# A two-layer hybrid attention kernel: the context side's modulation sums and one gate move from VectorE to GpSimd

## The chip, the cores and the metric

The kernel runs on one core of a Trainium2 chip. A core has TensorE (matmuls, PE in the profile, with its weight loads as PEld), VectorE (DVE), ScalarE (ACT), GpSimd (POOL), and SyncE (SP), which here issues nearly all transfers between HBM and SBUF. Each engine works through its own queue in order and waits for the others by semaphores. The metric is the device time of one execution in microseconds; less is better.

## The reference

Two layers of a backbone over 512 latent tokens and 256 context tokens of width 2048. Each layer first turns a conditioning vector into a shift, a scale and a gate, for the latent tokens from `c` and for the context tokens from `c_ctx`:

```python
sc = silu(c); scc = silu(c_ctx)
for l in range(2):
    shift, scale, gate       = split(sc  @ w_ada[l] + b_ada[l], 3)   # w_ada[l]: 2048 x 6144
    shift_c, scale_c, gate_c = split(scc @ w_ada[l] + b_ada[l], 3)
    h  = rms(x,  norm_w[l]) * (1 + scale)   + shift
    hc = rms(xc, norm_w[l]) * (1 + scale_c) + shift_c
    # h, hc -> one input projection -> three attention groups -> y (gated by silu(z))
    x = x + gate * (y @ w_out[l])
    if l == 0:
        xc = xc + gate_c * (y_c @ w_out[l])
return x
```

Everything is float32. The second layer's context output is never needed, so its `gate_c` is not either: layer 1 needs a shift and a scale for both sides, and a gate for the latent side alone.

## The kernel before, in words

Most of the time goes into matmuls with weights that stream from HBM: 128-row weight tiles land in `ws`, are split into a rounded high part `wh` (ScalarE, line 232) and the rest `wl` (VectorE, line 238), and three products of high and low parts approximate a float32 product (line 327). Between these projections the attention units run: scores into the PSUM tile `S`, a softmax over VectorE (lines 271, 276, 255) and ScalarE, transposes (line 330), and the product with the values. A `g` is a PSUM bank, `s` (tag `s3`) a large SBUF tile, `tm` and `sm` are temporaries.

The order of all instructions is made by a planner, in Python, while the program is built. Each strand of work is a generator (`Fiber`) with a priority; `Weaver` advances a clock of its own, every helper (`stt`, `ts`, `act`, `pmul`, ...) adds its estimated cost to its engine's clock with `bump`, and `gate` holds a strand until its instruction would start within 1.35 us (`AHEAD`). The result is one fixed order per engine. At run time the engines follow that order, whatever the real durations are.

The modulation of a layer is a product of one vector with a 2048 x 6144 matrix, for two vectors (sides 0, latent, and 1, context). The first layer's shift and scale are computed with TensorE (`ada_blocks`, line 734). All the rest goes through `ada_vec`: a chunk is 512 columns of `w_ada`, and an item is 128 rows of it, a tile `wa` of 128 x 512 (256 KB, two buffers). For each item and each side, VectorE multiplies `wa` by the side's activated conditioning `scT[:, k, m]` (one number per partition) and adds it into an accumulator `ac` (two buffers): a tensor_scalar (line 253) for the first of the 16 items of a chunk, a scalar_tensor_tensor (line 260) for the other 15. At the chunk's end TensorE sums over the partitions, with the accumulator as weights and a column of ones (line 792). After each item the strand pauses for `PACE` = 4 us of the planner's time.

`ada_rest` runs three such pieces one after the other at the lowest of the side priorities: layer 0's gate (4 chunks, both sides), layer 1's shift and scale (8 chunks, both sides), layer 1's gate (4 chunks, side 0). That is 16 chunks, 256 items and 448 VectorE instructions. Layer 1's shift and scale are wanted when layer 1 normalises its input; its gate is wanted by its output projection (`post_out`), near the end.

GpSimd has little to do: constants at the start, small transfers (line 308), and elementwise products (`pmul`, line 281): attention output times the silu gate, `s<-ot,s`, and two in the rotary embedding.

Of the kernel before, what the change touches and what calls it, by code (L numbers as in the profile page):

```python
# [138 lines left out]
class Kern:  # L139
# [139 lines left out]
    def pmul(self, out, a, b):  # L279
        yield from self.gate("pool")  # L280
        self.nc.gpsimd.tensor_tensor(out, a, b, op=OP.mult)  # L281
        self.w.bump("pool", 0.1 + 0.0035 * self.n(out))

    def load(self, out, in_, b=262144):

# [323 lines left out]
def body(K):  # L609
# [144 lines left out]
        K.put("tm", a)  # L754
        yield from ada_use(l, c0, n, pt, (0, 1))

    def ada_vec(l, c0s, sides):


        n = 512  # L760
        items = [(c0, k) for c0 in c0s for k in range(KT)]
        pend = deque()
        nxt = 0
        for c0 in c0s:
            acc = []
            for k in range(KT):
                while nxt < len(items) and (not pend or K.free("wa")):
                    w.cur.ft = w.vt
                    s = yield from K.get("wa")
                    c_, k_ = items[nxt]  # L770
                    nxt += 1
                    ts = yield from K.load_ahead(s, t["w_ada"][l, k_ * 128:(k_ + 1) * 128, c_:c_ + n])
                    pend.append((s, ts))
                s, ts = pend.popleft()
                yield from K.wait(ev_c)
                w.cur.ft = max(w.vt, ts)
                if k == 0:
                    for _ in sides:
                        acc.append((yield from K.get("ac")))
                for a, m in zip(acc, sides):  # L780
                    sc = scT[:, k, m:m + 1]
                    if k == 0:
                        yield from K.ts(a, s, sc, OP.mult, fast=True)
                    else:
                        yield from K.stt(a, s, sc, a, OP.mult, OP.add)
                K.put("wa", s)
                yield w.vt + PACE
            pt = yield from K.get("g")
            yield from K.sync()
            for c in range(n // 128):  # L790
                for a, m in zip(acc, sides):
                    nc.tensor.matmul(pt[:, 2 * c + m:2 * c + m + 1], a[:, c * 128:(c + 1) * 128], one,  # L792
                                     start=c == 0 and m == sides[0], stop=c == n // 128 - 1 and m == sides[-1],
                                     skip_group_check=True)
            w.pe(0.21 * n // 128 * len(sides))
            K.put("ac", *acc)
            w.spawn(ada_use(l, c0, n, pt, sides), 1, w.cur.ft)
# [24 lines left out]

    def ada_gate(l):
        sides = (0, 1) if l == 0 else (0,)
        yield from ada_vec(l, [2 * D + c for c in range(0, D, 512)], sides)
        yield from K.wait(*ev_gb[l])
        ps = yield from K.get("g")
        yield from K.sync()
        for m in sides:
            K.tr(ps[:KT, m * 128:(m + 1) * 128], ada[l][:, 32:48, m])  # L830
        w.pe(0.2)
        g = yield from K.get("tm")
        yield from K.act(g[:KT, :128 * len(sides)], ps[:KT, :128 * len(sides)])
        K.put("g", ps)
        for m in sides:
            yield from K.store(gscr[l][m], g[:KT, m * 128:(m + 1) * 128], 8192)
        K.put("tm", g)
        K.set(ev_gate[l])
# [1182 lines left out]

    def ada_rest():
        yield from ada_gate(0)
        yield from ada_vec(1, [c + o for c in range(0, D, 512) for o in (0, D)], (0, 1))
        yield from ada_gate(1)

    w.spawn(modulation(), 3)
# [69 lines left out]
```

## Time and profile before

| What | Value |
|---|---|
| Time, median of 3 runs | 2949.91 us (2947.4 to 2950.17) |
| Profiled execution: its own time | 2949.59 us |
| Profiled execution: span | 2947.8 us |
| TensorE busy | 2826.9 us (96%) |
| VectorE busy | 2025.8 us (69%) |
| ScalarE busy | 1243.7 us (42%) |
| GpSimd busy | 144.8 us (5%) |
| First and last accumulation into `ac` | 184.3 and 1634.0 us |
| Granted TensorE clock, mean | 0.99 |

The 1.8 us between the span and the execution's own time lie around the program. A row of the groups reads: line, engine, operation, output and inputs by name, shape, count, then busy time, mean of one in ns, and the idle time of the engine before them with what ended it. In the chain of work that ended last, each step is followed back to what released it; its shares tell through which lines the end of the kernel was reached. Layer 0 fills about the first 1700 us, layer 1 the rest.

### The profile page before, as it was taken

Reading aid. Unit: us, or ns where it says so; the run is one execution under the profiler, and the core shown is the slowest. Engines: PE = TensorE matmul, PEld = TensorE weight load, DVE = VectorE, ACT = ScalarE, POOL = GpSimd, SP = SyncE. Lnnn points to the kernel's source line nnn. Section 1 sums busy time; section 2 is a strip of 40 time slices with the busy share of each in tenths; the row PEclk is TensorE's granted clock in tenths of the full one; section 3 lists DMA queues with packets and bytes.
Section 4 is the critical chain, followed back from the end, with each engine's and each line's share of the span. In section 5 each row is a group of like instructions: output and inputs, shape, how many; then the busy total and the mean of one; then the engine's idle time right before and its main releaser. Section 6 shows DMA issues by size and latency. Waiting matters only on the chain.

```text
span 2947.8 us, 56481 instructions
## 1 busy us (share of the span) xinstructions
PE 2826.9 (96%) x21402; PEld 2715.2 (92%) x21402; DVE 2025.8 (69%) x5275; ACT 1243.7 (42%) x2714; POOL 144.8 (5%) x189
## 2 busy tenths in 40 slices
PE   5999999999989999889999999999999999999998
PEld 3779999999989999879999999999998999889998
DVE  5247787786987888889855374656657676489643
ACT  4223443342543454546421164444444455356421
POOL 3000000000100001000000000000000000000000
PEclk9999999999989999999999999999999999999999
DMA  9864444434323335424445343333231323412254
GB/s 254 251 203 129 120 122 116 121 109 117 101 85 106 90 111 154 149 83 129 164 140 168 113 128 86 92 96 89 71 99 46 90 61 102 132 45 88 93 160 127
DMA packets 423600, 349.19 MB, mean 118 GB/s; under 512 B 66260, under 2 KB 370178, under 8 KB 423328
## 3 DMA queue, kind: packets, MB, share of 16 engines
q1 hardware_dynamic: 421456, 344.27, 39.6%
q0 software_dynamic: 1872, 1.32, 0.5%
q8 instruction: 168, 2.75, 0.4%
q14 instruction: 104, 0.85, 0.1%
HBM read 303.97 MB, written 32.07 MB: 114 GB/s over the span
## 4 chain that ended last, share of the span: by engine, by line
PE 81%; DVE 11%; DMA 4%; issue 2%; SPq 1%; ACT 1%; DVEq 0%; ACTq 0%
PE g L327 67%; PE S L327 6%; PE g L330 5%; DVE wl L238 2%; DMA s<-w_ada 2%; SPq L297 1%; DVE s L271 1%; DVE s L238 1%; DVE ac L260 1%; DVE pt L238 1%; PE g L792 1%; DVE tm L238 1%; DVE s L260 1%; DVE s L255 1%; ACT s L232 1%
## 5 line engine op out<-in xcount | busy, mean ns | idle before, releaser
L327 PE MATMUL g<-wh,s 128*128 128x256 f32 (+1 forms) x9064 | 1766.7, 288 | 18.7 <-DVE tm L238 6.5
L327 PEld LDWEIGHTS g<-wh,s 128*128 128x128 f32 x9064 | 1457.7, 192 | 28.9 <-issue 9.1
L327 PE MATMUL g<-wl,s 128*128 128x256 f32 (+1 forms) x4532 | 1295.7, 286 | 6.5 <-DVE wl L238 6.3
L327 PEld LDWEIGHTS g<-wl,s 128*128 128x128 f32 x4532 | 870.7, 192 | 10.8 <-DVE wl L238 9.5
L238 DVE TENSOR_TENSOR wl<-ws,wh 128x512 fp32r<-128x512 f32 (+1 forms) x598 | 410.6, 687 | 455.6 <-PE g L327 262.7
L232 ACT ACTIVATE wh<-ws 128x512 fp32r<-128x512 f32 (+2 forms) x606 | 372.0, 615 | 415.5 <-PE g L327 383.7
L327 PE MATMUL g<-s,wh 128*128 128x384 f32 (+1 forms) x1600 | 453.4, 358 | 1.1 <-DVE s L238 0.6
L232 ACT ACTIVATE s<-s,sm 128x640 f32<-128x640 f32 (+3 forms) x260 | 195.9, 753 | 391.7 <-DVE sm L271 313.4
L260 DVE SCALAR_TENSOR_TENSOR ac<-wa,scT,ac 128x512 f32<-128x512 f32 x420 | 311.7, 760 | 9.2 <-DMA wa<-w_ada 8.3
L327 PEld LDWEIGHTS g<-s,wh 128*128 128x128 f32 x1600 | 294.3, 189 | 25.0 <-issue 2.1
L327 PE MATMUL g<-s,wl 128*128 128x384 f32 (+1 forms) x736 | 261.7, 356 | 0.0
L330 PE MATMUL g<-ident,s 128*128 128x128 f32 x1520 | 234.3, 279 | 20.1 <-DVE s L255 10.3
L327 PE MATMUL S<-s,s 128*128 128x256 f32 (+2 forms) x1260 | 240.6, 320 | 12.1 <-DVE sm L271 11.2
L232 ACT ACTIVATE tm<-g 128x512 f32<-128x512 f32 (+4 forms) x298 | 146.6, 513 | 226.3 <-PE g L327 126.8
L238 DVE TENSOR_TENSOR pt<-g,pt 128x512 fp32r<-128x512 f32 (+1 forms) x338 | 196.8, 591 | 65.0 <-ACT pt L232 63.8
L327 PE MATMUL g<-pt,s 128*128 128x256 f32 (+1 forms) x1348 | 223.0, 289 | 12.7 <-DVE pt L238 7.9
L232 ACT ACTIVATE pt<-g 128x512 fp32r<-128x512 f32 (+1 forms) x338 | 168.7, 516 | 142.4 <-PE g L330 134.7
L327 PEld LDWEIGHTS S<-s,s 128*128 128x128 f32 x1260 | 188.9, 191 | 27.1 <-DVE sm L271 17.9
L330 PEld LDWEIGHTS g<-ident,s 128*128 128x128 f32 x1520 | 179.7, 143 | 33.0 <-DVE s L255 13.7
L327 PEld LDWEIGHTS g<-pt,s 128*128 128x128 f32 x1348 | 188.8, 193 | 22.1 <-DVE pt L238 12.8
L281 POOL TENSOR_TENSOR s<-ot,s 64x256 f32<-64x256 f32 x100 | 87.3, 873 | 1976.9 <-DVE ot L238 1943.1
L327 PEld LDWEIGHTS g<-s,wl 128*128 128x128 f32 x736 | 139.3, 189 | 9.4
(155 smaller groups left out, 2226.3 us busy)
## 6 DMA issues: line engine op xcount, KB each, us to landing
wa<-w_ada SPq DMA_DIRECT2D x256, 256.0 KB
ws<-w_in SPq DMA_DIRECT2D x328, 128.0 KB
ws<-w_in SPq DMA_DIRECT2D x160, 256.0 KB
ws<-w_out SPq DMA_DIRECT2D x136, 256.0 KB
s<-w_ada SPq DMA_DIRECT2D x128, 256.0 KB
s<-scr SPq DMA_DIRECT2D x36, 384.0 KB
ws<-w_in SPq DMA_DIRECT2D x64, 192.0 KB
ws<-w_qb SPq DMA_DIRECT2D x54, 192.0 KB
```

Of the source, the lines that this page charges most:

```text
L232: self.nc.scalar.activation(out, in_, func, bias=bias, scale=scale, **kw)
L238: self.nc.vector.tensor_tensor(out, a, b, op=op)
L255: self.nc.vector.tensor_scalar(out, a, s1, s2, op0=op0, op1=op1)
L260: self.nc.vector.scalar_tensor_tensor(out, a, s, b, op0=op0, op1=op1)
L271: self.nc.vector.tensor_tensor_reduce(out, a, b, -1.0, init, OP.add, OP.min, acc)
L281: self.nc.gpsimd.tensor_tensor(out, a, b, op=OP.mult)
L297: self.nc.sync.dma_start(out, in_)
L327: self.nc.tensor.matmul(out, l, r, start=start, stop=stop, skip_group_check=True)
L330: self.nc.tensor.transpose(out, in_, self.ident)
L792: nc.tensor.matmul(pt[:, 2 * c + m:2 * c + m + 1], a[:, c * 128:(c + 1) * 128], one, start=c == 0 and m == sides[0], stop=c == n // 128 - ...
```

## The change

`ada_vec` takes a further argument, `pool`: the sides whose sums GpSimd computes. GpSimd gets no fused multiply-add here. For such a side, the first item of a chunk is one tensor_scalar into the accumulator (`pts`); each of the other 15 is a tensor_scalar that multiplies the tile `wa` in place, and a tensor_tensor that adds it to the accumulator (`padd`). Side 0, which reads the same tile, comes before it in program order, so the in-place product waits for VectorE's read. In layer 0's gate and in layer 1's shift and scale, side 1 goes to GpSimd; in layer 1's gate, which has only side 0, that side does. A `wa` buffer is now free for its next load when the later of both engines is done with it. In `ada_rest`, layer 1's gate waits until layer 1's input is complete.

```diff
+    def padd(self, out, a, b):
+        yield from self.gate("pool")
+        self.nc.gpsimd.tensor_tensor(out, a, b, op=OP.add)
+        self.w.bump("pool", 0.2 + 0.0025 * self.n(out))
+
+    def pts(self, out, a, s, op):
+        yield from self.gate("pool")
+        self.nc.gpsimd.tensor_scalar(out, a, s, None, op0=op)
+        self.w.bump("pool", 0.2 + 0.0025 * self.n(out))
...
-    def ada_vec(l, c0s, sides):
+    def ada_vec(l, c0s, sides, pool):
...
-                w.cur.ft = max(w.vt, ts)
                 if k == 0:
                     for _ in sides:
                         acc.append((yield from K.get("ac")))
+                end = t0 = max(w.vt, ts)
                 for a, m in zip(acc, sides):
+                    w.cur.ft = t0
                     sc = scT[:, k, m:m + 1]
-                    if k == 0:
+                    if m in pool:
+                        w.cur.ft = end
+                        yield from K.pts(s if k else a, s, sc, OP.mult)
+                        if k:
+                            yield from K.padd(a, a, s)
+                    elif k == 0:
                         yield from K.ts(a, s, sc, OP.mult, fast=True)
                     else:
                         yield from K.stt(a, s, sc, a, OP.mult, OP.add)
+                    end = max(end, w.cur.ft)
+                w.cur.ft = end
                 K.put("wa", s)
                 yield w.vt + PACE
...
-        yield from ada_vec(l, [2 * D + c for c in range(0, D, 512)], sides)
+        yield from ada_vec(l, [2 * D + c for c in range(0, D, 512)], sides, (1 - l,))
...
-        yield from ada_vec(1, [c + o for c in range(0, D, 512) for o in (0, D)], (0, 1))
+        yield from ada_vec(1, [c + o for c in range(0, D, 512) for o in (0, D)], (0, 1), (1,))
+        yield from K.wait(*(e for p in ev_in[1] for e in p))
         yield from ada_gate(1)
```

The planner makes a new order from this. First, VectorE in the first chunk of layer 0's gate, before:

```order
L260 SCALAR_TENSOR_TENSOR ac<-wa,scT,ac 128x512
L238 TENSOR_TENSOR s_2017<-s_2019,s_2016 128x256
L260 SCALAR_TENSOR_TENSOR ac<-wa,scT,ac 128x512
L260 SCALAR_TENSOR_TENSOR s_1946<-tm,g 128x384
L238 TENSOR_TENSOR wl<-ws,wh 128x512
L260 SCALAR_TENSOR_TENSOR s_1946<-tm,g 128x384
L260 SCALAR_TENSOR_TENSOR ac<-wa,scT,ac 128x512 x2
```

and in the changed program:

```order
L260 SCALAR_TENSOR_TENSOR ac<-wa,scT,ac 128x512
L238 TENSOR_TENSOR s_2017<-s_2019,s_2016 128x256
L260 SCALAR_TENSOR_TENSOR s_1946<-tm,g 128x384
L238 TENSOR_TENSOR wl<-ws,wh 128x512
L260 SCALAR_TENSOR_TENSOR s_1946<-tm,g 128x384
L260 SCALAR_TENSOR_TENSOR ac<-wa,scT,ac 128x512
```

One accumulation of the two of each item is gone from VectorE's order; what stands between is the same. Second, GpSimd in the changed program, where layer 1 begins: the last pair of the modulation, layer 1's small transfers, and the first items of its gate.

```order
L291 TENSOR_SCALAR wa<-wa,scT 128x512
L286 TENSOR_TENSOR ac<-ac,wa 128x512
L318 DMA colA<-qn_a 64x1 x2
L318 DMA colA<-kn_a 64x1 x2
...
L318 DMA sink<-sink_b 128x12
L291 TENSOR_SCALAR ac<-wa,scT 128x512
L291 TENSOR_SCALAR wa<-wa,scT 128x512
L286 TENSOR_TENSOR ac<-ac,wa 128x512
```

Before, no accumulation stood in this queue, and the gate's items came ahead of layer 1. Third, TensorE's sums over the partitions, the fifteenth chunk before:

```order
L327 MATMUL g<-wh,s_17638 128x256
L327 MATMUL g<-wl,s_17638 128x256
L327 MATMUL g<-wh,s_17639 128x256
L792 MATMUL g<-one,ac 128x1 x4
L327 MATMUL g<-wh,s_17635 128x256
```

and the twelfth and the thirteenth chunk of the changed program:

```order
L337 MATMUL g<-wl,s_17524 128x256
L337 MATMUL g<-wh,s_17525 128x256
L810 MATMUL g<-one,ac 128x1 x8
L337 MATMUL g<-wh,s_17527 128x256
...
L337 MATMUL g<-wl,s_21820 128x256
L337 MATMUL g<-wh,s_21821 128x256
L810 MATMUL g<-one,ac 128x1 x4
L337 MATMUL g<-wh,s_21789 128x256
```

The twelfth chunk, the last of layer 1's modulation, ends where the fifteenth ended before, and the gate's first chunk ends some 1900 rows later, in layer 1. The projections and attention units themselves stand in nearly the same places in TensorE's order, shifted by some tens of rows.

## The prediction

> **What bounds the kernel now.** I read the page first (busy time, then the chain of work that ended last), then the chain stage by stage, then the groups of the two accumulators, then GpSimd's own rows.
>
> ```profile
> span 2947.8 us, 56481 instructions
> PE 2826.9 (96%) x21402; PEld 2715.2 (92%) x21402; DVE 2025.8 (69%) x5275; ACT 1243.7 (42%) x2714; POOL 144.8 (5%) x189
> PE 81%; DVE 11%; DMA 4%; issue 2%; SPq 1%; ACT 1%; DVEq 0%; ACTq 0%
> ```
>
> TensorE is busy for 96% of the span and is 81% of the chain. VectorE is 69% busy, but only 11% of the chain runs through it. A microsecond taken from VectorE is therefore worth something only where the chain runs through VectorE. The sums that move lie between 184 and 1636 us; this is what each engine does there.
>
> ```profile
> core 0: us, PE busy (x) PEld busy (x) DVE busy (x) ACT busy (x) POOL busy (x), PEclk, DMA share, GB/s
> 184.00:721.00 537.00, 530.99 (x4060) 525.07 (x4057) 398.49 (x976) 198.75 (x434) 26.38 (x28) 1.00 0.42 120
> 721.00:910.00 189.00, 178.01 (x1309) 173.59 (x1308) 166.11 (x461) 88.14 (x224) 16.02 (x19) 0.95 0.32 94
> 910.00:1195.00 285.00, 277.11 (x2063) 273.75 (x2061) 237.49 (x632) 132.80 (x308) 32.23 (x39) 0.99 0.42 123
> 1195.00:1395.00 200.00, 181.80 (x1251) 170.71 (x1252) 185.96 (x554) 108.98 (x262) 1.06 (x2) 0.97 0.35 107
> 1395.00:1563.00 168.00, 161.02 (x1285) 158.14 (x1284) 113.65 (x246) 63.54 (x124) 3.22 (x5) 0.98 0.50 158
> ```
>
> Two stretches stand out. From 721 to 910 VectorE is busy for 166 of 189 us, from 1195 to 1395 for 186 of 200, and there alone TensorE has real gaps (11 and 18 us). The chain by line, for 184 to 1563 and for these two stretches:
>
> ```profile
> by line: PE g L327 63.1%; PE S L327 5.5%; PE g L330 5.3%; DVE ac L260 2.8%; DVE wl L238 2.3%; DVE s L271 2.2%; DVE s L238 2.2%; issue 1.8%; PE g L792 1.7%; DVE pt L238 1.5%; DVE s L255 1.3%; ACT s L232 1.2%; DVE s L260 1.1%; DVE tm L238 1.0
> by line: PE g L327 44.7%; DVE ac L260 7.1%; PE g L330 6.4%; DVE s L271 5.4%; PE S L327 5.1%; DVE wl L238 4.1%; DVE pt L238 3.7%; DVE s L255 3.3%; issue 3.3%; DVE tm L238 3.0%; PE g L792 2.6%; ACT s L232 1.6%; DVE ot L238 1.6%; DVE s L238 1.
> by line: PE g L327 25.0%; DVE s L238 9.9%; DVE ac L260 7.5%; DVE wl L238 6.5%; PE S L327 6.2%; PE g L330 5.0%; DVE s L260 4.9%; DVE s L271 4.9%; issue 4.8%; DVE pt L238 4.1%; DVE s L255 3.3%; DVE sm L260 2.7%; DVE sm L265 2.6%; ACT s L232 2
> ```
>
> The accumulations into `ac` are 2.8% of 1379 us, so 38.6 us of the chain, 13.4 us in the first stretch and 15.0 us in the second. That is all of their VectorE time (over 300 us) that the end of the kernel can feel today.
>
> **The change, part by part.** *What leaves VectorE.* The two groups:
>
> ```profile
> L260 DVE SCALAR_TENSOR_TENSOR ac<-wa,scT,ac x420: 730/746/1509, 189.6 to 1634.0; 128x512 f32<-128x512 f32 x140
> L253 DVE TENSOR_SCALAR ac<-wa,scT x28: 475/482/954, 184.3 to 1565.5; 128x512 f32<-128x512 f32 x28
> 184.00:721.00 537.00, 9.21 (x80) 9.45 (x81) 138.15 (x192) 1.00 0.42 120
> 721.00:910.00 189.00, 5.36 (x32) 5.33 (x33) 46.61 (x64) 0.95 0.32 94
> 910.00:1195.00 285.00, 5.88 (x52) 6.08 (x52) 70.71 (x96) 0.99 0.42 123
> 1195.00:1395.00 200.00, 3.38 (x30) 3.32 (x30) 34.82 (x48) 0.97 0.35 107
> 1395.00:1563.00 168.00, 1.90 (x16) 1.95 (x16) 23.34 (x32) 0.98 0.50 158
> ```
>
> (The last five rows are the stage view again, for instructions on `ac` alone; the third bracket counts VectorE's.) The context side of layer 0's gate (4 chunks of 16 items) and of layer 1's modulation (8 chunks), and layer 1's gate (4 chunks) are 16 chunks: 16 tensor_scalars and 240 scalar_tensor_tensors, 16 x 0.482 + 240 x 0.746 = 187 us of 2026. Before 1563 us the old kernel does 432 such instructions; the new one keeps 192 there (the latent side of 12 chunks), since by the order the twelfth chunk now ends where the fifteenth ended. So 240/432 = 56% of the 38.6 us can leave the chain: at most 21.5 us, at least nothing, if what comes next on the chain is only just behind. VectorE's other rows are ahead of TensorE in much of this time, so I take 18.
>
> *What GpSimd gets.* 256 tensor_scalars and 240 tensor_tensors of 128x512, which the old trace does not show. The nearest rows:
>
> ```profile
> L281 POOL TENSOR_TENSOR s<-ot,s 64x256 f32<-64x256 f32 x60 | 55.5, 925 | 1004.4 <-DVE ot L238 977.8 <-DVE sm L276 10.4 <-DVE sm L255 7.4
> L281 POOL TENSOR_TENSOR tm<-tm,rowB 128x384 f32<-128x384 f32 x8 | 8.7, 1093 | 39.6 <-ACT tm L232 39.6
> L281 POOL TENSOR_TENSOR tm<-tm,row_kk 128x256 f32<-128x256 f32 x4 | 3.2, 814 | 0.1
> L1998 POOL CAST maskB<-s 128x384 bf16<-128x384 f32 x1 | 0.5, 507 | 6.1 <-DMA s<-k_maskB 6.1
> ```
>
> (The first three are for 184 to 1195 us.) From 256 to 384 elements a tensor_tensor grows by 279 ns, so 512 give 1.37 us with the waits in it; undisturbed ones take 1.02 us at 384 (below), so I take 1.30. The tensor_scalar has one tensor to read: from the cast, 0.507 x 512/384 = 0.68 us below, the two-input 1.30 us above; nearer the cast, 0.7. In layer 0, 12 chunks give 192 x 0.7 + 180 x 1.3 = 368 us of GpSimd in 1379, a share of 27% beside the 6% it has. It has room; a pair of 2.0 us fits easily between items some 7 us apart. Were both 1.3 us, the share would be 35%.
>
> *What GpSimd costs VectorE.* The two engines get in each other's way today. Here are GpSimd and VectorE in the same few microseconds:
>
> ```profile
> 701.02 1.02 POOL L281 TENSOR_TENSOR tm<-tm,rowB 128x384 f32<-128x384 f32 x1 [32.62 <-ACT tm L232]
> 702.39 1.42 POOL L281 TENSOR_TENSOR tm<-tm,rowB 128x384 f32<-128x384 f32 x1 [0.35 <-ACT tm L232]
> 699.39 1.41 DVE L260 SCALAR_TENSOR_TENSOR ac<-wa,scT,ac 128x512 f32<-128x512 f32 x2
> 702.20 2.17 DVE L260 SCALAR_TENSOR_TENSOR ac<-wa,scT,ac 128x512 f32<-128x512 f32 x2
> ```
>
> The same GpSimd instruction takes 1.02 and then 1.42 us, and two accumulations that took 1.41 us before it take 2.17: each engine stood still for a while beside the other. On average, with GpSimd at work (184 to 1195) and with it idle (1410 to 1840):
>
> ```profile
> L260 DVE SCALAR_TENSOR_TENSOR ac<-wa,scT,ac 128x512 f32<-128x512 f32 x330 | 244.8, 764 | 7.3 <-DMA wa<-w_ada 6.6
> L238 DVE TENSOR_TENSOR wl<-ws,wh 128x512 fp32r<-128x512 f32 x173 | 122.0, 705 | 86.3 <-issue 57.8 <-PE g L327 16.4 <-ACT wh L232 2.7
> ...
> L238 DVE TENSOR_TENSOR wl<-ws,wh 128x512 fp32r<-128x512 f32 x96 | 66.2, 689 | 111.4 <-PE g L327 77.9 <-issue 26.0 <-ACT wh L232 6.3
> L260 DVE SCALAR_TENSOR_TENSOR ac<-wa,scT,ac 128x512 f32<-128x512 f32 x45 | 33.6, 746 | 1.9 <-DMA wa<-w_ada 1.7
> ```
>
> That is 18 and 16 ns per instruction, at a GpSimd share of (55.5 + 8.7 + 3.2)/1011 = 6.7%: 0.25 us for a share of one. At 27% it is 68 ns, and as the new instructions are some 1.3 times as long as the old ones, up to 90; I take 80 ns. Not every VectorE instruction pays; I count those that read two SBUF tensors, and tensor_scalars from SBUF to SBUF (the one on `ac` has a longest of 954 ns against a median of 482, so these wait too). On the chain from 184 to 1563 the lines `wl`, `s` L238, `s` L255 and `tm` are 6.8%, 94 us at about half a microsecond each, so 190; the remaining accumulations and the many small ones on `sm` (2.7% of 200 us at about 0.17 us are 32 in the second stretch alone) bring it to about 300. 300 x 0.08 = 24 us added, 20 if the others of a waiting set were later anyway.
>
> The Trainium skill ("SBUF — State Buffer", Who interferes with whom) states a rule against this change: VectorE and GpSimd share one pair of SBUF ports as an exclusive lock, taken by VectorE for two SBUF inputs or a two-port mode, and the second to come waits for the whole instruction. The 0.76 us that VectorE lost at 702, and the 0.40 us that GpSimd lost, agree with it.
>
> *The later gate.* Its 64 loads of 256 KB, 64 pairs on GpSimd and 16 small matmuls move from 1302-1636 to the matmuls that ran at about 1740-2043.
>
> ```profile
> by line: PE g L327 80.9%; PE g L330 5.5%; PE S L327 2.6%; DMA tm<-scr 1.8%; DMA tm<-x 1.7%; DVE wl L238 1.4%; issue 1.4%; PE g L1372 0.8%; DVE s L238 0.7%; SPq L297 0.6%; DVE s L260 0.4%; DVE tm L238 0.4%; PE g L792 0.4%; DVE pt L238 0.2%;
> ```
>
> From 1563 to 2050 lock-taking lines are about 2.5% of 487 us, some 20 instructions; GpSimd's share is there 123/300 = 41%, so 20 x 0.12 = 2.5 us more. The transfers `tm<-x` on this chain (1.7%, 8 us) share the queues with the gate's loads today; I give the move 2 us back. The gate's result is needed only by layer 1's output projection, at 2500 and later.
>
> *Buffers and queues.* `wa` has two buffers, and each is now free only after GpSimd's add. SP issues in order, so a late add would hold a weight load behind it. The planner reckons 2 x (0.2 + 0.0025 x 512) = 2.96 us for a pair that I put at 2.0, so it gives 0.96 us for waits; I cost this at nothing. The one-column matmuls L792 wait for GpSimd's last add: 16 ends, covered by the same margin; without it, a late microsecond at each end would cost TensorE 16 us. The gating products of attention (L281) now queue behind a pair, by up to 2 us; the planner counts this.
>
> **The sum.** -18 + 20 + 2.5 - 2 = +2.5 us on the profiled execution's own 2949.59 (1.8 us lies around the span): 2952, against a median of 2949.91 it is no difference. About 0.2% (5.9 us) is what a measurement here can tell from no change.
>
> **Rivals.** *No change* (forecast): 2946 to 2956. Chance 0.36.
>
> *The relief arrives, the lock costs little.* The new pairs come right after the latent side's accumulation on the same engine, at a moment when VectorE often has nothing urgent, and the planner, which knows of the lighter VectorE, places urgent work earlier. Then -21.5, a third of the lock's 24 us, and 2 us from the transfers: -15, 2935. For it: chain lines of VectorE are a tenth of the time outside the two stretches. Against: VectorE stands at 88 and 93% in them. Chance 0.32.
>
> *The lock decides: slower.* A tensor_scalar on GpSimd takes 1.3 us too, the share is 35%, and the mean wait grows with the length: 0.25 x 0.35 x 1.7 = 0.15 us on 300 instructions is 45 us, less 18, with 5 us in layer 1: +32; half of it hidden, +16. Time 2966 to 2982. Its place is 1195 to 1395, where 35 us of `ac` halve but every other instruction waits; it decides from a pair of 2.4 us, or when `wl` takes more than 0.8 us on average. The planner knows nothing of these waits, so TensorE's order leaves no room for them. Chance 0.26.
>
> *GpSimd late for its own consumers: slower.* Blocked by VectorE, a pair takes over 3 us, SP holds weight loads behind `wa`, and L792 waits: 12 to 16 ends at 2 us are up to 32 us, 2980. The two-microsecond slack of the pair speaks against it. Chance 0.06.
>
> **From these the numbers.** Faster 0.32, same 0.36, slower 0.32. The likeliest case alone is 2946 to 2956; as both signs hold most of the chance, the range runs to the middle of the faster and of the slower case: 2932 to 2974.
>
> **What would show it.** Right: VectorE's busy time falls by less than 187 us, by some 187 - 100; `wl` takes about 0.77 us on average before 1563; GpSimd is busy for about 640 us; `ac` on the chain falls to about 17 us while `wl`, `s` and `sm` gain as much. Wrong towards faster: `wl` stays near 0.70 us, and the gaps of TensorE in 721-910 and 1195-1395 (29 us together) close by half. Wrong towards slower: SP's or TensorE's waits for GpSimd's adds, or pairs over 2.4 us.

## The result: 1% slower

| | before | changed |
|---|---|---|
| Time, median of 4 runs each on the same chip | 2950.04 us (2947.4 to 2954.57) | 2980.55 us (2977.82 to 2984.5) |
| Profiled execution, its own time | 2949.59 us | 2984.5 us |

The ratio is 1.0104 (95% interval 1.0090 to 1.0118): 30.5 us slower, against a forecast of 2952 and a range up to 2974. The page of the changed kernel: span, busy times, and the two large new groups on GpSimd (POOL).

```profile
span 2982.3 us, 57007 instructions
PE 2838.3 (95%) x21402; PEld 2715.0 (91%) x21402; DVE 2001.9 (67%) x5019; ACT 1243.9 (42%) x2714; POOL 901.2 (30%) x685
...
L291 POOL TENSOR_SCALAR wa<-wa,scT 128x512 f32<-128x512 f32 x240 | 404.6, 1686 | 696.4 <-DVE ac L260 423.3
...
L286 POOL TENSOR_TENSOR ac<-ac,wa 128x512 f32<-128x512 f32 x240 | 322.8, 1345 | 19.6
```

VectorE (DVE) lost 256 instructions, and its busy time fell by 24 us, from 2025.8 to 2001.9. GpSimd is busy for 901 us, not the 640 foreseen: a pair takes 1.69 + 1.35 = 3.03 us. The tile view of `ac` gives the shortest, the median and the longest of one (ns), and when they ran:

```profile
L286 POOL TENSOR_TENSOR ac<-ac,wa x240: 1262/1295/1843, 190.1 to 2069.3; 128x512 f32<-128x512 f32 x120
L291 POOL TENSOR_SCALAR ac<-wa,scT x16: 1565/1570/1977, 182.4 to 1996.1; 128x512 f32<-128x512 f32 x16
```

The add is 1.30 us, as taken. The tensor_scalar is 1.57 us at the median, more than twice what I took, so a pair has 2.87 us even without waits. Where VectorE's time went is seen in its groups, by shape, before:

```profile
L238 DVE TENSOR_TENSOR wl<-ws,wh 128x512 fp32r<-128x512 f32 x544 | 380.7, 700 | 442.9 <-PE g L327 253.4 <-issue 130.4 <-ACT wh L232 29.9
L238 DVE TENSOR_TENSOR pt<-g,pt 128x512 fp32r<-128x512 f32 x258 | 174.1, 686 | 54.8 <-ACT pt L232 53.9
...
L255 DVE TENSOR_SCALAR s<-s,sm 128x640 f32<-128x640 f32 x80 | 44.4, 555 | 1.6
...
L238 DVE TENSOR_TENSOR sm<-sm 128x1 f32<-128x1 f32 x120 | 19.9, 166 | 25.6 <-ACT sm L232 25.0
```

and in the changed kernel:

```profile
L238 DVE TENSOR_TENSOR wl<-ws,wh 128x512 fp32r<-128x512 f32 x544 | 414.6, 762 | 480.8 <-PE g L337 285.8 <-issue 118.3 <-ACT wh L232 35.4
L238 DVE TENSOR_TENSOR pt<-g,pt 128x512 fp32r<-128x512 f32 x258 | 173.4, 684 | 53.9 <-ACT pt L232 52.9
L260 DVE SCALAR_TENSOR_TENSOR ac<-wa,scT,ac 128x512 f32<-128x512 f32 x180 | 136.7, 760 | 1.7 <-DMA wa<-w_ada 1.3
L255 DVE TENSOR_SCALAR s<-s,sm 128x640 f32<-128x640 f32 x80 | 53.0, 662 | 2.1
...
L238 DVE TENSOR_TENSOR sm<-sm 128x1 f32<-128x1 f32 x120 | 31.1, 259 | 37.3 <-ACT sm L232 36.6
```

`wl`, which reads two SBUF tensors, went from 700 to 762 ns. That is the mean over the whole kernel, and the pairs run only up to 2071 us. The same group from 184 to 1563 us alone, before and then changed:

```profile
L238 DVE TENSOR_TENSOR wl<-ws,wh 128x512 fp32r<-128x512 f32 x212 | 148.8, 702 | 108.8 <-issue 67.3 <-PE g L327 26.3 <-ACT wh L232 5.7
```

```profile
L238 DVE TENSOR_TENSOR wl<-ws,wh 128x512 fp32r<-128x512 f32 x211 | 173.7, 823 | 143.2 <-issue 64.0 <-PE g L337 54.0 <-ACT wh L232 12.6
```

So beside the pairs it takes 823 ns, and after 2080 us, without them, 700 again. Even a two-input instruction on one column (`sm`) went from 166 to 259 ns over the whole kernel. `pt<-g,pt`, which has one of its two inputs in PSUM (`g`), didn't change. One such place in the timeline (start, duration, engine; the bracket is idle time before):

```profile
1242.36 0.55 DVE L238 TENSOR_TENSOR wl<-ws,wh 128x384 fp32r<-128x384 f32 x1
...
1243.67 1.56 POOL L291 TENSOR_SCALAR wa<-wa,scT 128x512 f32<-128x512 f32 x1 [9.33 <-DVE ac L260]
1243.82 0.74 DVE L260 SCALAR_TENSOR_TENSOR s<-g,colC,s 128x512 fp32r<-128x512 f32 x1
...
1244.66 0.59 DVE L255 TENSOR_SCALAR sm<-sm 128x6 f32<-128x6 f32 x1
1245.29 0.17 DVE L253 TENSOR_SCALAR sm<-sm 128x6 int32<-128x6 int32 x1
1245.32 1.27 POOL L286 TENSOR_TENSOR ac<-ac,wa 128x512 f32<-128x512 f32 x1
1245.40 1.61 DVE L238 TENSOR_TENSOR wl<-ws,wh 128x384 fp32r<-128x384 f32 x1
...
1247.06 0.44 PE L337 MATMUL g<-wl,s 128*128 128x384 f32 x1 [1.34 <-DVE wl L238]
```

GpSimd's product ends at 1245.23; a VectorE tensor_scalar of six elements per partition, begun 1.0 us behind it, ends then too, after 0.59 us (its neighbour on as many takes 0.17). The add ends at 1246.59; `wl`, which took 0.55 us when it ran 3 us earlier, takes 1.61 us and ends 0.42 us behind the add, and the matmul that wants it starts late. The instruction on `g` at 1243.82 runs beside GpSimd undisturbed.

**Where the time arises.** The three products run the same 18732 matmuls on one line (327 before, 337 after), so I aligned the traces on the n-th of them. Each column is a kernel's time minus before's time at the same matmul, in us; the last four are experiments, told of below:

| before's time | changed | e1, no pairs | e10, sums on VectorE | e8, gate on VectorE | e3, only the gate later |
|---|---|---|---|---|---|
| 912 | +1 | -18 | -8 | +2 | +1 |
| 1395 | +8 | -36 | -11 | +9 | 0 |
| 1700 | +11 | -39 | -11 | +11 | -9 |
| 1800 | +20 | -38 | -6 | +13 | -6 |
| 2100 | +32 | -30 | +3 | +22 | +3 |
| 2939 | +35 | -32 | +1 | +21 | +3 |

In the changed kernel, 11 us come before 1700 and 22 us (unrounded) between 1700 and 2100, where layer 1's gate now lies. The stage view (columns as in the prediction; the third bracket is VectorE's, the fifth GpSimd's), first the old row for the stretch that the prediction gave only as a chain, then the changed kernel's:

```profile
1563.00:2050.00 487.00, 482.58 (x3810) 469.68 (x3809) 274.67 (x685) 193.12 (x381) 8.84 (x12) 1.00 0.38 108
```

```profile
721.00:910.00 189.00, 173.75 (x1292) 168.17 (x1291) 159.46 (x409) 87.57 (x221) 86.78 (x66) 0.98 0.28 82
...
1195.00:1395.00 200.00, 179.62 (x1196) 167.14 (x1196) 181.84 (x500) 103.66 (x248) 69.36 (x45) 0.96 0.32 99
...
1563.00:2050.00 487.00, 469.77 (x3684) 455.56 (x3685) 278.58 (x618) 178.91 (x345) 199.11 (x146) 0.99 0.45 131
```

TensorE's gaps did not close: 15 us from 721 to 910 (11 before) and 20 us from 1195 to 1395 (18 before), though VectorE does some 50 instructions fewer in each. From 1563 to 2050 it does 67 fewer in more time, and TensorE's gaps grow from 4 to 17 us. (These are windows of each kernel's own time; between the same matmuls the changed kernel's gaps are 15, 21 and 16 us, to the same conclusion.) The chain of waits of this trace could be followed over only two fifths of its span, so I don't set its shares beside those of before.

### The profile page after: what moved, and what is told of

Same layout as the page of the kernel before. It is cut to its first block, busy times and chain, and to the rows that moved or that the text cites. A ratio compares the mean times of both kernels' runs of the same rounds, so it can differ in the third digit from the quotient of the medians.

```text
span 2982.3 us, 57007 instructions
## 1 busy us (share of the span) xinstructions
PE 2838.3 (95%) x21402; PEld 2715.0 (91%) x21402; DVE 2001.9 (67%) x5019; ACT 1243.9 (42%) x2714; POOL 901.2 (30%) x685
## 3 DMA queue, kind: packets, MB, share of 16 engines
q0 software_dynamic: 1872, 1.32, 0.4%
## 5 line engine op out<-in xcount | busy, mean ns | idle before, releaser
L238 DVE TENSOR_TENSOR wl<-ws,wh 128x512 fp32r<-128x512 f32 (+1 forms) x598 | 447.0, 748 | 494.7 <-PE g L337 296.5
L291 POOL TENSOR_SCALAR wa<-wa,scT 128x512 f32<-128x512 f32 x240 | 404.6, 1686 | 696.4 <-DVE ac L260 423.3
L232 ACT ACTIVATE s<-s,sm 128x512 f32<-128x512 f32 (+3 forms) x260 | 195.9, 754 | 424.8 <-DVE sm L271 346.1
L286 POOL TENSOR_TENSOR ac<-ac,wa 128x512 f32<-128x512 f32 x240 | 322.8, 1345 | 19.6
```

The costliest lines, as they stand in the source:

```text
L232: self.nc.scalar.activation(out, in_, func, bias=bias, scale=scale, **kw)
L238: self.nc.vector.tensor_tensor(out, a, b, op=op)
L286: self.nc.gpsimd.tensor_tensor(out, a, b, op=OP.add)
L291: self.nc.gpsimd.tensor_scalar(out, a, s, None, op0=op)
```

## The experiments

My theory after the result was the prediction's third case: GpSimd's pairs make VectorE wait, and the order leaves no room for it ("the lock"). Its rivals: the later place of layer 1's gate, the new order by itself, and GpSimd being late for its own consumers. The diffs of e4, e5, e6 and e3 are against the kernel before, all others against the changed kernel.

**The pairs left out (e1).** The order of the changed kernel, without the 240 pairs.

```diff
-                        yield from K.pts(s if k else a, s, sc, OP.mult)
                         if k:
-                            yield from K.padd(a, a, s)
+                            for _ in range(2):
+                                yield from K.gate("pool")
+                                w.bump("pool", 0.2 + 0.0025 * n)
+                        else:
+                            yield from K.pts(a, s, sc, OP.mult)
```

> The changed program in its own order, with GpSimd's 240 pairs left out (only the first tensor_scalar of each chunk stays), so the context side's modulation and layer 1's gate are sums of one item only. Theory 'lock' (VectorE stands still while GpSimd reads SBUF): without the pairs VectorE's relief is all that is left, and the time falls below the kernel before, to 2930-2945 us; VectorE is busy for 187 us less than before, wl back at 0.69 us on average. Theory 'place' (the new order, with the gate in layer 1, is what costs): the order is that of the changed kernel, so the time stays at 2965 us or more. Theory 'late consumers' (buffers of wa held, TensorE's one-column sums waiting for GpSimd): as 'lock' in time, 2940 us, but wl's average is then no different in the changed kernel.

Measured: 2918.19 us against 2951.4, ratio 0.9887 (0.9872 to 0.9902). Busy times of its page, one group by shape (as above), and two rows of the stage view:

```profile
PE 2816.5 (97%) x21402; PEld 2710.0 (93%) x21402; DVE 1872.3 (64%) x5019; ACT 1244.1 (43%) x2714; POOL 174.8 (6%) x205
```

```profile
L238 DVE TENSOR_TENSOR wl<-ws,wh 128x512 fp32r<-128x512 f32 x544 | 382.4, 703 | 499.5 <-PE g L337 273.0 <-issue 131.3 <-ACT wh L232 37.1
```

```profile
721.00:910.00 189.00, 184.29 (x1420) 180.93 (x1419) 148.60 (x434) 93.96 (x238) 20.55 (x22) 0.99 0.32 89
...
1195.00:1395.00 200.00, 188.08 (x1323) 178.90 (x1321) 180.67 (x537) 117.57 (x274) 1.94 (x1) 0.97 0.36 116
```

With the same order and without the pairs, the gaps do close, to 5 and 12 us (5 and 11 between the same matmuls), and the kernel is 62 us faster than with them, faster even than the lock theory had it. VectorE is busy for 1872.3 us with the same 5019 instructions that take 2001.9 in the changed kernel: the pairs make it wait for 130 us. The relief alone is 33 us, more than the 21.5 that I had called the most.

**The gate not held back (e2).** The changed kernel without the wait for layer 1's input.

```diff
-        yield from K.wait(*(e for p in ev_in[1] for e in p))
```

> The changed kernel, with layer 1's gate directly after the modulation again, still on GpSimd. Of the 34 us that the changed kernel loses, 21 arise between 1700 and 2100 us, where that gate runs. Theory 'place': those 21 us go, about 2960 us. Theory 'lock': the gate's pairs meet VectorE wherever they stand; starting at about 1570 us they overlap the output projection of layer 0, where VectorE is lighter, and the start of layer 1: 2965 to 2978 us.

Measured: 2993.09 us against 2951.4, ratio 1.0141 (1.0126 to 1.0156), slower than the changed kernel; both expectations missed. Aligned as above it stands at +18 at 1700, +35 at 1750 and +45 from 1900 to the end. The place is seen in GpSimd's timeline, then in those of SyncE (SPq) and ScalarE, then in TensorE's:

```profile
1737.24 1.13 POOL L318 DMA_DIRECT2D colA<-qn_a  x2
...
1752.99 0.55 POOL L318 DMA_DIRECT2D sink<-sink_b  x1 [0.51 <-issue]
1753.57 1.60 POOL L291 TENSOR_SCALAR wa<-wa,scT 128x512 f32<-128x512 f32 x1
1755.25 1.26 POOL L286 TENSOR_TENSOR ac<-ac,wa 128x512 f32<-128x512 f32 x1
```

```profile
1756.54 0.34 SPq L307 DMA_DIRECT2D wa<-w_ada  x1
1756.98 0.89 SPq L307 DMA_DIRECT2D ws<-w_in  x2
...
1760.56 0.63 ACT L232 ACTIVATE wh<-ws 128x512 fp32r<-128x512 f32 x1 [8.14 <-DMA ws<-w_in]
```

```profile
1764.14 2.89 PE L340 MATMUL g<-ident,s 128*128 128x128 f32 x12 [9.36 <-DVE s L238]
```

The waits of SyncE from 1735 to 1765 us (total, times, longest) name what held it:

```profile
SPq L307 <- POOL ac L286: 10.7, 2, 10.3
```

Layer 1's small transfers, some of which wait for the landing of others, hold GpSimd's queue from 1737 to 1753 us, in the midst of the gate's pairs. (In the kernel before they were issued between 1165 and 1440 us; in the changed kernel from 1564 to 1580, between two pieces of the sums.) The pair behind them ends at 1756.5, and only then is its `wa` buffer free. SyncE waits for that for 10.3 us, and behind the load of `wa` stand weight loads. ScalarE waits 8.1 us for these, VectorE's `wl` for ScalarE, and TensorE stands still for 9.4 us at 1764. Behind that gap its granted clock is 0.80 from 1760 to 1800 us, against 1.00 from 1800 to 1850. So with the sums on GpSimd, an early gate is worse, for a reason that neither theory had: it is the prediction's fourth rival, GpSimd late for its own consumers.

**The pairs added to the old order (e4).** Before's order on every other engine, all sums on VectorE; GpSimd does an unused pair for each item.

```diff
+                sc = scT[:, k, sides[-1]:sides[-1] + 1]
+                nc.gpsimd.tensor_scalar(dum, s, sc, None, op0=OP.mult)
+                if k:
+                    nc.gpsimd.tensor_tensor(dum, dum, dum, op=OP.add)
```

> The kernel before, in its own order on all other engines, with GpSimd doing idle work beside it: for each of the 256 items a tensor_scalar of the tile wa into a spare tile and, but for a chunk's first, a tensor_tensor on the spare tile. VectorE still makes all sums. Theory 'lock': no relief, the whole price: 20 to 60 us over the kernel before, 2970 to 3010 us, wl at 0.75 us or more on average. Theory 'late consumers': the tiles wa are held until GpSimd has read them, so some of the loss shows too, but with wl at 0.70 us. Theory 'place': no loss, 2950 us.

Measured: 3030.94 us against 2951.4, ratio 1.0271 (1.0254 to 1.0288), +80 us, more than the lock theory's 20 to 60. Busy times of its page, and two groups by shape:

```profile
PE 2866.2 (95%) x21402; PEld 2735.0 (90%) x21402; DVE 2170.4 (72%) x5275; ACT 1244.7 (41%) x2714; POOL 888.6 (29%) x685
```

```profile
L788 POOL TENSOR_SCALAR dum<-wa,scT 128x512 f32<-128x512 f32 x256 | 461.5, 1803 | 557.2 <-DMA wa<-w_ada 547.8
```

```profile
L260 DVE SCALAR_TENSOR_TENSOR ac<-wa,scT,ac 128x512 f32<-128x512 f32 x420 | 366.6, 890 | 6.8 <-DMA wa<-w_ada 6.2
```

Work that nobody waits for except through the two `wa` buffers costs 80 us, with VectorE busy for 145 us more. Part of it falls on the accumulations themselves (760 to 890 ns), which here begin together with the pair, as soon as the tile has landed.

**GpSimd busy, but not reading (e5).** As e4, with memsets in place of the pair; a copy of one column at each end holds the buffer `wa`.

```diff
+                nc.gpsimd.tensor_copy(dum[:, :1], s[:, :1])
+                for _ in range(5 if k else 3):
+                    nc.gpsimd.memset(dum, 0.0)
+                nc.gpsimd.tensor_copy(dum[:, :1], s[:, :1])
```

> As the redundant kernel, but GpSimd's work per item reads next to nothing: one column of wa copied, five memsets of a 128x512 spare tile (three for a chunk's first item), one column of wa copied again, so the tile is held about as long and GpSimd is about as busy. Theory 'lock by reads': 2948 to 2955 us, no difference to the kernel before, wl at 0.70 us. Theory 'lock by any access', or 'late consumers': as the redundant kernel, 2970 us or more.

Measured: 2966.27 us against 2951.4, ratio 1.0047 (1.0030 to 1.0064), +15 us, between the two expectations. The same two views:

```profile
PE 2838.5 (96%) x21402; PEld 2721.6 (92%) x21402; DVE 2048.1 (69%) x5275; ACT 1245.1 (42%) x2714; POOL 977.0 (33%) x1949
```

```profile
L789 POOL MEMSET dum<- 128x512 f32 x1248 | 669.6, 537 | 72.2
```

```profile
L238 DVE TENSOR_TENSOR wl<-ws,wh 128x512 fp32r<-128x512 f32 x544 | 379.6, 698 | 423.7 <-PE g L327 248.3 <-issue 120.9 <-ACT wh L232 27.2
...
L255 DVE TENSOR_SCALAR s<-s,sm 128x640 f32<-128x640 f32 x80 | 47.9, 599 | 1.6
```

GpSimd is busier than with the pairs, and `wl` has its 698 ns; the loss is a fifth of e4's. So most of the cost is not that GpSimd works, holds the buffers or fills its queue, but that it reads.

**The sums left out of the old order (e6).** The 240 accumulations of the last side are left out of the kernel before, with its order.

```diff
+                    elif m == sides[-1]:
+                        yield from K.gate("dve")
+                        w.bump("dve", 0.07 + 0.06 + 0.00104 * n)
```

> The kernel before in its own order, with the 240 scalar_tensor_tensors that the change moves left out (the context side's modulation and layer 1's gate are then sums of one item), the planner still reckoning them; nothing is added on GpSimd. In the changed order, without its pairs, the kernel was 33 us faster than before, more than the 21.5 us that the chain of waits was taken to allow. Theory 'the chain is no bound' (an instruction that is off the chain in one run delays others that are on it): about 30 us here too, 2917 to 2925. Theory 'the new order brought the rest': 15 to 21 us, 2930 to 2936.

Measured: 2936.49 us against 2949.03, ratio 0.9957 (0.9942 to 0.9972): a relief of 12.5 us, within the bound that I had from the chain. The new order gets 33 us (e1) out of the same omission; there the planner knew of the lighter VectorE.

**ScalarE makes the product (e7).** The product in place moves to ScalarE, the add stays on GpSimd.

```diff
-                        yield from K.pts(s if k else a, s, sc, OP.mult)
+                        yield from K.act(s if k else a, s, scale=sc)
```

> The changed kernel with the product of each pair on ScalarE (an activation that scales the tile in place) instead of GpSimd's 1.57 us tensor_scalar; GpSimd keeps the 1.30 us add. Theory 'lock': GpSimd's reading time falls from 754 to about 320 us, so of the 62 us that the pairs cost, 45% stay, 28 us: 2940 to 2955 us; wl averages about 0.725 us. ScalarE gets 160 us more, and is 42% busy. Theory 'late consumers': a third engine in each item makes it later, not earlier: 2980 or more.

Measured: 2975.92 us against 2949.03, ratio 1.0095 (1.0080 to 1.0111), where the lock theory said 2940 to 2955. Busy times, and groups by shape of VectorE and of ScalarE (ACT):

```profile
PE 2838.8 (95%) x21402; PEld 2715.6 (91%) x21402; DVE 1951.5 (66%) x5019; ACT 1403.6 (47%) x2970; POOL 469.0 (16%) x429
```

```profile
L238 DVE TENSOR_TENSOR wl<-ws,wh 128x512 fp32r<-128x512 f32 x544 | 403.9, 743 | 472.8 <-PE g L337 295.3 <-issue 89.0 <-ACT wh L232 41.9
```

```profile
L232 ACT ACTIVATE wa<-wa,scT 128x512 f32<-128x512 f32 x240 | 173.5, 723 | 286.1 <-issue 127.6 <-DVE ac L260 114.1 <-DMA wa<-w_ada 25.9
```

VectorE's waits fall from 130 to 79 us (1951.5 - 1872.3), but hardly any time is won, and both expectations missed: ScalarE is busy for 160 us more in a queue that also makes `wh`, and stood idle for another 114 us before these products, waiting for VectorE's accumulation. What part each has is not told apart.

**The same with a spare tile (e9).** So that ScalarE needn't wait for VectorE, its product goes to a tile of its own.

```diff
+    spare = K.st([128, 512], name="spare")
...
-                        w.cur.ft = end
-                        yield from K.pts(s if k else a, s, sc, OP.mult)
+                        yield from K.act(spare if k else a, s, scale=sc)
                         if k:
-                            yield from K.padd(a, a, s)
+                            yield from K.padd(a, a, spare)
```

> As the kernel with the product on ScalarE, but into a spare tile instead of in place, so ScalarE no longer waits for VectorE's reading of the same tile (114 us of its idle time there). Theory 'lock plus ScalarE's waits': the waits go and the lock of 320 us of adds stays: 2950 to 2965 us. Theory 'ScalarE is simply too busy to take 174 us': 2970 to 2980 us, no difference.

Measured: 2973.05 us against 2950.04, ratio 1.0073 (1.0054 to 1.0092): 3 us less than e7, within the range of the second theory. Groups by shape of VectorE and of ScalarE:

```profile
L260 DVE SCALAR_TENSOR_TENSOR ac<-wa,scT,ac 128x512 f32<-128x512 f32 x180 | 171.4, 952 | 5.4 <-DMA wa<-w_ada 4.8
```

```profile
L232 ACT ACTIVATE spare<-wa,scT 128x512 f32<-128x512 f32 x240 | 172.9, 720 | 108.4 <-DMA wa<-w_ada 101.0 <-POOL ac L286 6.6
```

ScalarE's wait for VectorE is gone, and one for the transfer stands in its place (101 us). GpSimd's add now meets the same item's accumulation on VectorE: 952 ns instead of 760. VectorE's busy time is 1999.6 us, as in the changed kernel, though GpSimd reads for less than half as long. In the changed kernel the product in place, which waits for that accumulation, kept these two apart.

**Layer 1's gate back on VectorE (e8),** still late; the context's sums stay on GpSimd.

```diff
-        yield from ada_vec(l, [2 * D + c for c in range(0, D, 512)], sides, (1 - l,))
+        yield from ada_vec(l, [2 * D + c for c in range(0, D, 512)], sides, (1,))
```

> The changed kernel with only the context side on GpSimd; layer 1's gate is summed on VectorE, still beginning with layer 1. Theory 'lock': of the 21 us lost between 1700 and 2100 us, the 12 that the kernel without pairs does not lose go, less a little for 48 us more on VectorE there: 2968 to 2974 us. Theory 'place': they stay, 2980 us.

Measured: 2970.55 us against 2949.03, ratio 1.0079 (1.0062 to 1.0096), 10 us better than the changed kernel, as the lock theory had it. By the table it runs with the changed kernel to 1700 and gains its 10 us from there to 2100. **Both at once (e11),** e9 with the gate on VectorE:

> As the kernel with the spare tile, and layer 1's gate on VectorE, still beginning with layer 1: GpSimd adds 180 times instead of 240. Theory 'lock': a quarter less of the lock, and none in the dense stretch at 1740-2040: 5 to 8 us under the kernel with the spare tile, about 2945 to 2955, the nearest to a version that beats the kernel before. If it is not under the kernel with the spare tile, the gate's adds were not what cost there.

Measured: 2968.05 us against 2950.04, ratio 1.0059 (1.0042 to 1.0077): 5 us less than e9, as expected, at a level above what was expected.

**Only the gate's place (e3).** The kernel before, with layer 1's gate held back, on VectorE.

```diff
+        yield from K.wait(*(e for p in ev_in[1] for e in p))
         yield from ada_gate(1)
```

> The kernel before, all sums on VectorE, with layer 1's gate beginning with layer 1: the change's second part alone. Between 1302 and 1636 us VectorE is relieved of 48 us; the kernel without pairs gained 9 us between 1195 and 1395 and lost 9 between 1750 and 2050 beside the gate's loads. Theory 'place costs what it gives': 2945 to 2955 us. If it is 2940 or less, the placement is worth having alone; if 2960 or more, the later gate is a loss of its own.

Measured: 2951.42 us against 2949.03, ratio 1.0005 (0.9991 to 1.0018), as expected. By the table it gains 9 us by 1700, where the gate is gone, and has given them back by 2100, where it is now.

**Only the order (e10).** The changed kernel's order everywhere, but the moved sums run on VectorE where they are issued; the planner still counts them on GpSimd.

```diff
-                        yield from K.pts(s if k else a, s, sc, OP.mult)
+                        for _ in range(2 if k else 1):
+                            yield from K.gate("pool")
+                            w.bump("pool", 0.2 + 0.0025 * n)
                         if k:
-                            yield from K.padd(a, a, s)
+                            nc.vector.scalar_tensor_tensor(a, s, sc, a, op0=OP.mult, op1=OP.add)
+                        else:
+                            nc.vector.tensor_scalar(a, s, sc, None, op0=OP.mult)
```

> The changed kernel's order on every other engine, but all the moved sums are computed by VectorE after all, with the old instructions, at the places where the planner thinks of GpSimd; GpSimd gets none. Without any of these sums the changed order took 2918 us and the old order 2936. Theory 'the new order is better in itself': about 18 us under the kernel before, 2928 to 2936. Theory 'the order fits only a light VectorE' (its gain is that VectorE's urgent work is placed as if the sums were gone): the sums delay VectorE where the planner left no room, 2948 to 2965 us.

Measured: 2950.16 us against 2950.04, ratio 1.0000 (0.9989 to 1.0012). Busy times:

```profile
PE 2826.4 (96%) x21402; PEld 2709.4 (92%) x21402; DVE 2030.0 (69%) x5275; ACT 1243.4 (42%) x2714; POOL 142.1 (5%) x189
```

That is in the second theory's range. With the sums on VectorE, the new order costs nothing and gives nothing. The difference of 30 us to the changed kernel is that of where the sums run.

**The new order, GpSimd busy but not reading (e12).** e1 with four memsets and two copies of a column in place of each pair.

```diff
+                            nc.gpsimd.tensor_copy(dum[:, :1], s[:, :1])
+                            for _ in range(4):
+                                nc.gpsimd.memset(dum, 0.0)
+                            nc.gpsimd.tensor_copy(dum[:, :1], s[:, :1])
```

> The changed kernel's order on every other engine; in place of each pair, GpSimd copies one column of wa, sets a spare tile four times, and copies one column again, 2.7 us that read next to nothing; the 240 sums are left out. In this order no sums at all took 2918 us, GpSimd's pairs 2981. Theory 'the reading is the price': only what the idle kernel with memsets lost (15 us) comes on top of 2918: 2925 to 2938 us, wl at 0.70 us on average. Theory 'GpSimd busy or a tile held is the price, whatever it does': 2965 us or more.

Measured: 2926.61 us against 2948.75, ratio 0.9914 (0.9895 to 0.9932). Busy times, and `wl` by shape:

```profile
PE 2821.1 (96%) x21402; PEld 2711.5 (93%) x21402; DVE 1885.5 (64%) x5019; ACT 1244.2 (43%) x2714; POOL 820.3 (28%) x1645
```

```profile
L238 DVE TENSOR_TENSOR wl<-ws,wh 128x512 fp32r<-128x512 f32 x544 | 380.4, 700 | 499.4 <-PE g L337 287.6 <-issue 132.9 <-ACT wh L232 36.7
```

**Together.** One order on TensorE, ScalarE and SyncE, and the 240 sums in four ways:

| The 240 sums | Time | VectorE busy | GpSimd busy |
|---|---|---|---|
| left out (e1) | 2918 us | 1872 us | 175 us |
| left out, GpSimd writes as long (e12) | 2927 us | 1886 us | 820 us |
| on VectorE (e10) | 2950 us | 2030 us | 142 us |
| on GpSimd (the change) | 2981 us | 2002 us | 901 us |

VectorE does the sums for 32 us of the kernel's time. GpSimd does them for 62: some 8 come with a GpSimd that is as busy and holds `wa` about as long but hardly reads (e12), some 54 with the pairs proper, which read SBUF while VectorE wants to. In e12 nothing waits for GpSimd's result either; what that is worth was not measured apart, but VectorE's busy time, 1886 against 2002 us with the same 5019 instructions, shows where most of it falls. That the price falls in step with the time that GpSimd reads is not shown: e7 and e9 read for less than half as long and win some 5 and 8 us, with ScalarE busier by 160 us. None of the kernels that compute all sums is faster than the kernel before; e10 and e3 equal it.

## Why the prediction was wrong

*The forecast and the rivals.* "No change" didn't come. "The lock decides: slower" did, at the top of its 2966 to 2982, by the points that it named: it "decides from a pair of 2.4 us", and the pair takes 2.87 us undisturbed; "or when `wl` takes more than 0.8 us on average", and before 1563 us, the stretch for which the forecast gave 0.77, it takes 0.823. (The mean over the whole kernel, 0.762, hides that.) That its sum comes so near is partly luck: 45 + 5 for the lock and 18 of relief give +32, where 62 and 33 were measured. Both terms were too low by 12 to 15 us, and it then thought half of the +32 hidden. `wl` carries about a quarter of VectorE's loss (35 of 130 us, both widths, change against e1); as much falls on the short instructions on `sm`, and most of the rest on the tensor_scalars from SBUF to SBUF and on other two-input instructions.

*The price of the tensor_scalar: wrong.* Between the bounds 0.68 and 1.30 us I took 0.7, from a cast with one input. It takes 1.57 us, above the upper bound, longer than the two-input add. The cast lacked the number per partition that it multiplies with, and it wrote bf16; whether either is the reason was not tried. GpSimd's share in layer 0 was foreseen at 27% and 35%; its sums alone (lines 291 and 286 between 184 and 1563 us) make it (315.4 + 241.2)/1379 = 40%.

*The term "20 for the lock": mis-sized, the main error; this is the step that failed.* It counted 300 instructions on the chain at 80 ns and took 20 of the 24 us. By e1, the pairs cost 62 us of time: by the aligned traces 49 before 1700, for which the 20 were meant, and 13 from there to 2100, for which 2.5 were. First, the wait of one instruction was too small: with GpSimd's share at 40% in place of 27%, `wl` waits 121 ns (823 against 702), and 300 such waits would be 36 us. Second, what is left up to 49 must be more waits, or longer ones, than the 300 counted, and what a lower clock takes (below); these were not told apart. Seen over the whole kernel, VectorE waits 130 us instead of 100, and I let 24 of those 100 us reach the end, while 62 of 130 do. That share holds elsewhere: added VectorE time, added kernel time, from the page and the medians:

| | VectorE busy | time | share |
|---|---|---|---|
| waits: the change less e1 | +130 us | +62 us | 0.48 |
| waits: e4 less before | +145 us | +80 us | 0.55 |
| waits: e5 less before | +22 us | +15 us | 0.67 |
| work: e10 less e1 | +158 us | +32 us | 0.20 |
| work: before less e6 | +145 us | +12.5 us | 0.09 |

(The busy times are those of one profiled execution. That of e6 was its fastest, 2928.31 us; by it the last share would be 0.15. The e5 difference is small against the spread of its runs, 2958.79 to 2970.42. e7 and e9, where ScalarE is loaded too, are left out.) A microsecond of waiting cost about half a microsecond or more; a microsecond of the accumulations themselves a tenth to a fifth. The planner puts an accumulation where VectorE has time for it, but a wait falls on whatever VectorE does next to a pair, and on the instructions on `sm` that follow one upon another. That is how I read it; which instructions pass their wait on was not settled by a run. Part of the price isn't idle time: the mean granted clock of TensorE was 0.980 in e4's profile and 0.990 in that of before, and 1% of 3029 us would be some 30 of e4's 80 us (an estimate; 0.989 in the changed kernel and 0.991 in e1 would be 6 of the 62).

*"At most 21.5" of relief: right for the old order, wrong for the new.* Left out of the old order the sums give 12.5 us (e6). With an order made for a lighter VectorE they give 33 (e1), so the chain of the old trace bounds only what the old order could gain. The 18 that I took thus was too low by 15, in the other direction than the lock.

*VectorE's busy time, "187 - 100".* It fell by 24. The 187 was a sum of durations, and instructions that follow each other overlap: the durations of all VectorE groups add up to 2272 us before and 2085 in e1, 187 less, but the busy time, which counts an overlap once, falls by only 153.5 (2025.8 - 1872.3). Of these, 130 came back as waits.

*The later gate, "2.5 us more" and "2 us back": mis-sized.* The changed kernel loses 22 us between 1700 and 2100. With the gate on VectorE there (e8, e10, e3) 11, 14 and 12 us are lost in the same stretch too, and e10 and e3 had won as much before it: the place is neutral over the whole (e3, 1.0005). The other 10 us are GpSimd's 60 pairs at that place (e8 against the change).

*"GpSimd late for its own consumers": not seen in the changed kernel.* TensorE's waits name GpSimd nowhere. SyncE (SPq) waits for the adds as often as it waited for VectorE's accumulations, and somewhat longer (the waits by engine; total us, times, longest), after and then before:

```profile
SPq L307 <- POOL ac L286: 100.2, 57, 9.1
```

```profile
SPq L297 <- DVE ac L260: 81.2, 57, 6.1
```

What these waits cost was not measured apart. The planner's 2.96 us for a pair left not the 0.96 us of margin that I counted but 0.1, and with waits a pair takes 3.03; in the changed kernel that sufficed. In e2, where the transfers in GpSimd's queue came on top, it did not, and SyncE held weight loads behind `wa` as this rival has it.

*The mechanism was right.* The Trainium skill ("SBUF — State Buffer", Who interferes with whom) has it that VectorE with two SBUF inputs contends with a GpSimd instruction that reads SBUF, not with one that only writes, that VectorE's two-port forms, which a tensor_scalar can take, contend with GpSimd, and that an instruction with at most one SBUF input outside these forms does not. The rows here agree: `wl` at 762 ns in the changed kernel and 700 beside memsets (e12); the tensor_scalar 128x640 at 555 before, 662 in the changed kernel, and 599 beside memsets (e5); `pt` at 683 to 686 throughout. The Trainium skill ("Perfetto Trace Analysis", Optimizing Scalar/DVE Operations) says that offloading between these two engines "might not help"; here it cost 1.0%.

## What to carry to other kernels

Before moving VectorE work to GpSimd, price the GpSimd form by a run of exactly that form, and set VectorE's waits against the work taken from it: here 727 us of GpSimd pairs that read SBUF made VectorE wait 130 us, about half of that wait reached the end, and of the low-priority work taken away only a tenth to a fifth had reached it. The share of the old chain bounds what an edit can win only as long as the order stays; run the work left out, in the new order, to learn the most that a move can give. And a second engine's queue has other things in it: look at what stands ahead of the work that moves there and behind it (in e2, 16 us of small transfers held back a pair, and with it the weight loads). Take a mean over the stretch that a change touches: over the whole kernel `wl` lost 62 ns, beside the pairs 121.

## What was unexpected of the hardware

On GpSimd a 128x512 float32 tensor_scalar with a number per partition takes 1.57 us, an add of two tensors 1.30 us, a memset 0.54 us. A VectorE instruction of six elements per partition, otherwise 0.17 us, took 0.59 us beside a GpSimd product: a wait can be longer than what waits. GpSimd work that nearly only writes (e5: 670 us of memsets beside one-column copies of 0.3 us) left VectorE's two-input `wl` as it was (698 ns) and still lengthened its tensor_scalars from SBUF to SBUF (555 to 599 ns at 640 elements).
